# Grouped-query attention: a quarter of the score tiles get exp on VectorE, with the knot sum made by TensorE

## The chip, the cores and the metric

One core of a Trainium2 chip. The metric is the device time of one execution in microseconds; the number quoted for a kernel is the median of its runs. PE is TensorE, ACT is ScalarE, DVE is VectorE, POOL is GpSimd, SP is SyncE, whose queue issues DMAs. Differences between two changed kernels are of medians, and some of these come from different rounds; the kernel before ran in all of them, with medians from 545.3 to 547.2 us.

## The reference

```python
batch, n_q_heads, n_kv_heads, seq, head_dim = (8, 8, 2, 1024, 64)   # q, k, v: randn * 0.1, float32
for g in range(n_kv_heads):                       # 4 query heads share one k and v head
    scores = scale * q_group @ k_group.T          # scale = 1/8
    attn = exp(scores - scores.max(-1)); attn = attn / (attn.sum(-1) + 1e-08)
    output[:, q_start:q_end] = attn @ v_group
```

The inputs are small, so the scores are close to zero and the softmax is nearly uniform. A pass says little about how exact exp is.

## The kernel before

The work is cut into 64 units (batch, head pair, half of the queries) of 8 steps. A step is one chunk of 128 keys: PE makes its scores for two heads ("sides") in PSUM, ACT takes exp of three 512-column tiles at once, and ten steps later PE multiplies the result by V, with a column of ones appended that gives the softmax sum. V's matmuls use 64 key rows each, so that two of them (sides 0 and 1) run side by side in the array; half-way through a unit the sides swap, and a marker on SP's queue keeps the two row halves from touching one bank at once.

```python
    LAG = NKC + 2
    WIDTHS = (3, 3)                      # two score buffers of three banks
    def flush():
        pt = p_pool.tile([128, max(WIDTHS), QBS], BF16, name="pt")
        nc.scalar.activation(out=pt[...], in_=state["tile"][...], func=AF.Exp, scale=scale)
    def output_step(i):
        ...
        for c in (2 * part, 2 * part + 1):
            for qs in range(NQS):
                for rows in range(2):
                    side = rows ^ half
                    lo = rows * 64
                    mm = nc.tensor.matmul(ops[:, side, qs * (D + 1) : (qs + 1) * (D + 1)],
                        lhsT=pcell[(u * NKC + c, side)][lo : lo + 64, qs * 128 : (qs + 1) * 128],
                        rhs=vt[(b, side)][lo : lo + 64, c, :], ...)
        ...                              # end of a unit: reciprocal and multiply on DVE, from PSUM
        nc.vector.reciprocal(out=rec, in_=o[:, :, :, D])
        nc.vector.tensor_tensor(out=ost, in0=o[:, :, :, 0:D], in1=rec..., op=ALU.mult)
    # load_batch: GpSimd casts k and q to bf16 in DRAM, SP transposes them into SBUF by DMA (5 in a row)
```

The softmax here doesn't subtract the row's maximum and nothing guards it: scores larger than these inputs give would overflow.

## Time and profile before

| | before |
|---|---|
| median time | 546.68 us |
| ACT busy | 466.6 us (86%) |
| PE busy by the profile / at its real pace | 357.6 / about 240 us |
| DVE busy | 57.5 us |
| granted PE clock | 0.927 |

PE's list of waits (who waited, for whom: microseconds in all, how often, the longest):

```profile
PE sps L125 <- ACT pt L105: 99.8, 232, 1.1
PE ops L148 <- SPq L162: 36.1, 7, 10.4
PE ops L148 <- DVE ost L175: 22.8, 38, 1.0
```

PE mostly waits for ACT to free a score buffer. That is what a kernel bound by ACT looks like. The line of the normalisation (DVE ost) is small and its longest wait is 1.0 us: DVE has nothing else to do and serves at once.

### The profile page before, as it was taken

To read this page: it belongs to the slowest core of one execution; us is meant where nothing else is said; L and a number is where in the kernel's file an instruction comes from. 1 tells how busy PE (TensorE), PEld (TensorE's weight loads), DVE (VectorE), ACT (ScalarE), POOL (GpSimd) and SP (SyncE) were. 2 spreads that over 40 slices of the span, in tenths; PEclk is the share of its full clock that TensorE was granted. 3 is DMA by queue.
4 is the path that set the end of the run, shared out by engine and by line. 5 is a ranking of instruction groups with operands and counts; after the bars stand their busy time and mean duration, and the time that the engine had idled before them with its cause. 6 is when DMAs were issued, how large, how long until landed. Compare 5 with 4: busy or idle time off the path is not lost.

```text
span 545.4 us, 19767 instructions
## 1 busy us (share of the span) xinstructions
PE 357.6 (66%) x9216; PEld 228.7 (42%) x9216; DVE 57.5 (11%) x128; ACT 466.6 (86%) x343; POOL 98.2 (18%) x76
## 2 busy tenths in 40 slices
PE   0436766676748767587775767767674867767764
PEld 0024443444435444354443444444442544444443
DVE  0001011011101101011110110101110110111101
ACT  0547999699978999699996999959997899999994
POOL 8986100440007100080002600010000000000000
PEclk9988999699996999889996999869999699899999
DMA  9999923891159911698117921371114211111012
GB/s 75 156 149 157 157 45 69 114 132 40 32 111 97 97 41 43 117 115 83 40 33 127 132 47 41 68 109 41 41 37 99 45 39 41 41 42 40 22 41 61
DMA packets 209107, 41.13 MB, mean 75 GB/s; under 512 B 209024, under 2 KB 209024, under 8 KB 209024
## 3 DMA queue, kind: packets, MB, share of 16 engines
q0 software_dynamic: 99200, 12.59, 36.3%
q1 hardware_dynamic: 109824, 27.28, 26.0%
q8 instruction: 72, 1.18, 0.9%
q14 instruction: 11, 0.09, 0.1%
HBM read 25.17 MB, written 27.26 MB: 96 GB/s over the span
## 4 chain that ended last, share of the span: by engine, by line
ACT 45%; PE 21%; issue 13%; DVE 7%; SPq 7%; DMA 4%; POOL 3%; ACTq 0%; POOLq 0%
ACT pt L105 45%; PE ops L148 12%; PE sps L125 9%; SPq L81 6%; DVE ost L175 5%; DMA qscr<-in_q_dram 4%; POOL qscr L76 2%; DVE rec L173 2%; POOL kscr L67 1%; SPq L72 0%; POOL vs L86 0%; ACTq L105 0%; POOL vs L85 0%; SPq L162 0%; POOLq L215 0%
## 5 line engine op out<-in xcount | busy, mean ns | idle before, releaser
L105 ACT ACTIVATE pt<-sps 128x1536 bf16<-128x1536 f32 x342 | 465.3, 1472 | 70.8 <-PE sps L125 70.6
L125 PE MATMUL sps<-qT,kT 64*128 64x512 bf16 x1024 | 282.7, 410 | 121.4 <-ACT pt L105 99.8
L148 PEld LDWEIGHTS <-pt 64*128 64x128 bf16 x8192 | 217.0, 98 | 225.7 <-issue 83.8
L148 PE MATMUL ops<-vs,pt 64*128 64x65 bf16 x8192 | 260.0, 197 | 61.9 <-SPq L162 36.1
L125 PEld LDWEIGHTS <-kT 64*128 64x128 bf16 x1024 | 79.4, 99 | 86.4 <-issue 70.5
L76 POOL DMA_DIRECT2D qscr<-in_q_dram x32 | 72.0, 4055 | 3.8 <-DMA kscr<-in_k_dram 1.8
L173 DVE RECIPROCAL rec<-ops 128x8 f32<-128x8 f32 x64 | 13.3, 208 | 482.1 <-PE ops L148 482.1
L85 POOL MEMSET vs<- 128x8 bf16 x16 | 13.3, 833 | 251.3 <-PE ops L148 251.3
L175 DVE TENSOR_TENSOR ost<-ops,rec 128x512 f32<-128x512 f32 x64 | 44.2, 691 | 2.2
L67 POOL DMA_DIRECT2D kscr<-in_k_dram x8 | 16.5, 2058 | 0.9 <-POOLq L215 0.9
L86 POOL DMA_DIRECT2D vs<-in_v_dram x16 | 14.4, 897 | 9.6 <-POOL vs L85 5.9
L105 ACT ACT_TABLE_LOAD x1 | 1.3, 1283 | 0.7 <-PEq L215 0.7
L215 POOL MEMSET const-float32-0.0<- 128x1 f32 x1 | 0.1, 98 | 0.2 <-issue 0.2
L215 POOL MEMSET const-float32-1.0<- 128x1 f32 x1 | 0.1, 98 | 0.0
L215 POOL MEMSET const-bfloat16-1.0<- 128x1 bf16 x1 | 0.1, 98 | 0.0
L215 POOL MEMSET const-uint8-127<- 128x1 uint8 x1 | 0.1, 98 | 0.0
## 6 DMA issues: line engine op xcount, KB each, us to landing
out_dram<-ost SPq DMA_DIRECT2D x128, 128.0 KB, 2.2
qscr<-in_q_dram POOLq DMA_DIRECT2D x32, 256.0 KB, 12.6
kscr<-in_k_dram POOLq DMA_DIRECT2D x8, 256.0 KB, 6.2
vs<-in_v_dram POOLq DMA_DIRECT2D x16, 128.0 KB, 5.3
qT<-qscr SPq DMA_TRANSPOSE x32, 3.8
kT<-kscr SPq DMA_TRANSPOSE x8, 3.7
```

The source lines that it names most:

```text
L67: nc.gpsimd.dma_start(out=kscr.rearrange("s (g d) -> s g d", g=G), in_=k[b].rearrange("g s d -> s g d"),)
L76: nc.gpsimd.dma_start(out=qscr.rearrange("s (g d) -> s g d", g=G), in_=q[b, j::NPAIR].rearrange("g s d -> s g d"),)
L81: nc.sync.dma_start_transpose(out=qt, in_=qscr)
L85: nc.gpsimd.memset(vs[:, :, D], 1.0)
L86: nc.gpsimd.dma_start(out=vs[:, :, 0:D], in_=v[b, g].rearrange("(c p) d -> p c d", p=128),)
L105: nc.scalar.activation(out=pt[:, 0 : len(cells), :], in_=state["tile"][:, 0 : len(cells), :], func=AF.Exp, scale=scale,)
L125: nc.tensor.matmul(state["tile"][:, len(state["cells"]), :], lhsT=kT[b][side * D : (side + 1) * D, c * 128 : (c + 1) * 128], rhs=qT[(b, j) ...
L148: mm = nc.tensor.matmul(ops[:, side, qs * (D + 1) : (qs + 1) * (D + 1)], lhsT=pcell[(u * NKC + c, side)][lo : lo + 64, qs * 128 : (qs + 1) ...
L173: nc.vector.reciprocal(out=rec, in_=o[:, :, :, D])
L175: nc.vector.tensor_tensor(out=ost, in0=o[:, :, :, 0:D], in1=rec.unsqueeze(3).to_broadcast([128, G, NQS, D]), op=ALU.mult,)
L215: nc = _bacc.Bacc("TRN2", target_bir_lowering=False, num_devices=1)
```

## The change

The intent is to relieve ACT. On 4 of 15 steps DVE makes exp: one multiply-add turns the score into the bits of a bf16 number (so 2^x, linear between powers of two), written as uint16. Adding 32, 64 and 96 to those bits gives three more copies with shifted knots, and the weighted sum of the four is a much better exp. The sum costs no instruction of DVE: PE adds up four sets of output matmuls, each with its own weighted copy of V, which GpSimd prepares. Around this the change also makes the first transposes on PE, spreads the loads, uses score tiles of 1024 columns, and lets the output matmuls follow 15 steps behind, spread over 6.5 of 8 steps.

```diff
+KNOT_W = (1.0, 0.83984375, 0.70703125, 0.59375)
+KNOT_STEP = 32
-    LAG = NKC + 2
-    WIDTHS = (3, 3)
+    LAG = 15
+    GAP = 1.5
+    DVE_NUM, DVE_DEN = 4, 15
+    apool: 2 buffers of 2 banks (ACT);  dpool: 1 buffer of 2 banks (DVE);  ops: 2 banks      [summary]
+    def weigh_v(b, g):
+        for w in range(NK):
+            nc.gpsimd.tensor_scalar(out=vs[:, g, w, :, 0:D], in0=vf, scalar1=KNOT_W[w], ..., op0=ALU.mult)
+    def shift_knots():                   # for two DVE steps together
+        for w in range(1, NK):
+            nc.vector.tensor_scalar(out=pd[:, w, 0:n], in0=pd[:, 0, 0:n],
+                scalar1=float(w * KNOT_STEP), scalar2=None, op0=ALU.add)
     def score_step(i):
+        if not dve:
+            nc.scalar.activation(out=pt, in_=sps, func=AF.Exp, scale=scale)
+            pcell[i] = [pt]
+            return
+        nc.vector.tensor_scalar(out=pd[:, 0, n], in0=sps, scalar1=bits_scale, scalar2=bits_bias,
+            op0=ALU.mult, op1=ALU.add)
+        pcell[i] = [pd[:, w, n].bitcast(BF16) for w in range(NK)]
+        if n == 1:
+            shift_knots()
+    def output_items(u):
+        for half in range(2):
+            for c in range(NKC):
+                nk = NK if on_dve(u * NKC + c) else 1
+                items += [(half, c, w) for w in range(nk)]
+    # main loop: spread casts and transposes; score_step(i); then the output items due in step i;
+    # after the last item of a unit: reciprocal and multiply on DVE                           [summary]
```

## The prediction

> **What bounds the kernel now.** I read the page's totals first, then the groups, the waits of PE and ACT, the stretches by window, and the timeline of one good stretch, one batch change, and the end.
>
> ```profile
> PE 357.6 (66%) x9216; PEld 228.7 (42%) x9216; DVE 57.5 (11%) x128; ACT 466.6 (86%) x343; POOL 98.2 (18%) x76
> ...
> L105 ACT ACTIVATE pt<-sps 128x1536 bf16<-128x1536 f32 x342 | 465.3, 1472 | 70.8 <-PE sps L125 70.6
> ...
> L148 PE MATMUL ops<-vs,pt 64*128 64x65 bf16 x8192 | 260.0, 197 | 61.9 <-SPq L162 36.1
> L173 DVE RECIPROCAL rec<-ops 128x8 f32<-128x8 f32 x64 | 13.3, 208 | 482.1 <-PE ops L148 482.1
> L175 DVE TENSOR_TENSOR ost<-ops,rec 128x512 f32<-128x512 f32 x64 | 44.2, 691 | 2.2
> ```
>
> ACT does nothing but exp and is busy 466.6 of 545.4 us; it idles 70.8 us, all for scores from PE: 17.4 us of it before its first tile. DVE is busy for 11%. So exp on ACT bounds the steady stretch; some 53 us of stalls, about 19 us at the start and about 9 us at the end are added.
>
> ACT's pace, from its own timeline: seven tiles in one unbroken block.
>
> ```profile
> 19.41 9.51 ACT L105 ACTIVATE pt<-sps 128x1536 bf16<-128x1536 f32 x7 [17.39 <-PE sps L125]
> ```
>
> (9.51 - 1.47) / 6 = 1.34 us from start to start for 1536 columns: 0.833 ns a column and about 0.06 us fixed. The 1472 ns of the group is longer because neighbours overlap.
>
> PE's true pace also has to come from starts, since its ends are modelled. A good stretch (PE and its weight loads):
>
> ```profile
> 305.28 0.42 PE L148 MATMUL ops<-vs,pt 64*128 64x65 bf16 x16
> 305.50 0.10 PEld L125 LDWEIGHTS <-kT 64*128 64x128 bf16 x2
> 305.53 0.38 PE L125 MATMUL sps<-qT,kT 64*128 64x512 bf16 x2
> 305.53 0.50 PEld L148 LDWEIGHTS <-pt 64*128 64x128 bf16 x16
> 305.75 0.41 PE L148 MATMUL ops<-vs,pt 64*128 64x65 bf16 x16
> ```
>
> Sixteen output matmuls take 0.25 us (305.28 to 305.53), a pair of score matmuls 0.22 us (305.53 to 305.75). So PE's work is 512 steps x 0.47 = 240 us, far less than the 358 us "busy". A batch change shows what a PE stop costs:
>
> ```profile
> 292.49 0.62 PE L148 MATMUL ops<-vs,pt 64*128 64x65 bf16 x16 [3.76 <-SPq L162]
> 292.93 0.61 PE L125 MATMUL sps<-qT,kT 64*128 64x512 bf16 x2
> 293.33 0.65 PE L148 MATMUL ops<-vs,pt 64*128 64x65 bf16 x16
> ```
>
> After 3.76 us without work the same sixteen take 0.44 us and the pair 0.40; the stretches by window give a granted clock of 0.65, 0.50 and 0.83 from 290 to 305. The stop itself is the half-way marker of the output bank, which sits in SP's queue behind five DMA transposes of 1.25 us each.
>
> **What the Trainium skill says.** "TensorE: Matmul & The Clock Gate", HAM oscillation: an idle PE falls back to half clock; the trace agrees (0.50 above). "ScalarE: Activation LUTs", What ACT_TABLE_LOAD costs: 0.833 ns per element whatever the function; the trace agrees. "VectorE: DVE Perf Modes", The perf-mode tier table: a one-source 16-bit SBUF op of 2048 elements runs in the 4x mode in 693 ns, and a PSUM operand drops a tier; no run of before has such an op, so both figures for DVE are estimates. "SBUF — State Buffer", Who interferes with whom: a DVE op in a two-port mode and a GpSimd op lock each other out; before has no such DVE op.
>
> **The change, part by part.** 136 of 512 steps (a step is one key chunk of both heads, 128x1024 scores) go to DVE, 376 stay on ACT.
>
> *ACT.* One tile is now 1024 columns: 0.853 + 0.06 = 0.91 us. 376 x 0.91 = 343 us, from about 466: 120 us less.
>
> *DVE.* Conversion of 1024 columns from PSUM: the 128x512 multiply from PSUM takes 691 ns = 533 at one column a cycle + 158; for 1024, 1067 + 158 = 1.22 us. 136 x 1.22 = 166. Knot shifts: 68 groups x 3 x about 0.65 us (693 ns in isolation by the page, a little less back to back) = 133. Normalisation stays, 57.5. Sum about 357 us, from 57.5.
>
> *PE.* A DVE step needs four sets of output matmuls instead of one: 376 x 16 + 136 x 64 = 14720, from 8192. At the 64-in-1.04-us pace of the last unit's weight loads (16.2 ns each) that is 237 us, plus 512 x 0.22 = 113: 350 us at full clock, from 240.
>
> So the three engines stand at 343, 357 and 350 us. That is a balance on paper, but PE takes its instructions in order, ACT has two score buffers, DVE one, and there is one output bank pair; so what counts is what PE waits for.
>
> *The output turnover.* From the last output matmul of a unit to the first of the next: in the tail of before PE's last block ends at 537.41 (its last issue about 0.17 earlier), the reciprocal starts at 537.45, the multiply ends at 538.39, PE restarts at 538.44. That is 1.2 us of which two score pairs (0.44) of the new schedule fill a part, since the stream of output matmuls uses 6.5 of 8 steps. So 0.76 us of PE idle per unit, and per unit PE needs 14720/64 x 16.2 ns = 3.72 + 8 x 0.22 = 1.76: 5.48 + 0.76 = 6.24 us. ACT needs 5.36 us, DVE 5.6 us. PE's chain is the longest of the three.
>
> *The DVE queue in it.* DVE is in order too. If the second conversion of a pair has just been put in, the reciprocal waits behind a conversion and three shifts, 1.2 + 1.9 us. The pair's second step lies at steps 7 and 14 of 15, units end at step 6 of 8, so over 120 steps (15 units) every distance occurs twice: in the same step the reciprocal is about 2.6 us late, one step earlier 1.9, two 1.1, three 0.3, otherwise nothing. 2 x 5.9 / 15 = 0.8 us per unit on average if nothing absorbs it, and it comes in runs: about eight units with it, seven without.
>
> *Start.* K and the first Q come straight as fp32 and are transposed on PE in place of the cast to DRAM and the DMA transpose. 1 MB at the 157 GB/s seen in the first slices is 6.4 us, about 8.5 us with issue; then cast, 8 transposes, copy, about 3.5 us: first exp near 12.5 us instead of 19.4. The output stream starts 16.5 steps later, 11 us: about 24 us.
>
> *End.* Two units of output matmuls are left when scores are done: 2 x (3.7 + 1.2) = 10 us, and 3.6 us from the last multiply to the end as before.
>
> *Batch changes.* Transposes are spread four steps apart, so the marker no longer queues behind five of them; the 53 us of ACT stalls in the middle and the half clock after them go.
>
> *GpSimd.* 64 multiplies of 128x512 and the casts; busy for under a third of the span; can hold up a shift now and then, a few us.
>
> *Sum.* Without the DVE queue: 24 + 62 x 6.24 + 10 + 3.6 = 424 us. With all of it: 424 + 62 x 0.8 = 474 us. I take **445 us**, below the middle. The split at 4 of 15 and the stream's gap look chosen on a chip; if my queue were paid in full, fewer DVE steps would do better, so part of it is probably absorbed.
>
> **Rivals.**
> 1. *ACT or DVE stays the bound and the engines overlap nearly perfectly.* For: the sums of 343, 357 and 350 are so even, and the gap in the stream is about the turnover. 13 + 357 + 14 = 385 us. Against: PE in order, one output bank pair, one DVE score buffer; a step on DVE makes PE issue 0.22 + 0.52 us twice between two ACT tiles, 1.5 us, while ACT's two buffers allow little more than 1.1.
> 2. *PE's own clock.* Waits of 2.6 + 0.8 us come close to the 3.76 us that halved the clock in before. If each of some eight such places costs 5 us, and the mean clock stays near 0.93, PE's chain grows by 25 to 40 us: 485 to 500. For: the window table above. Against: two score pairs lie in the wait and PE is far denser elsewhere.
> 3. *The shifts don't run in the 4x mode* (uint16, with arithmetic), or GpSimd's lock holds them. At half rate a shift takes about 1.2 us, 204 of them 245 us, DVE 470 and with its waits about 510 us. Against: the skill's condition asks for 16-bit operands in SBUF with unit step, which these are.
> 4. *Nothing gained.* It would take rivals 2 and 3 together.
>
> **Range and chances.** The lower end, 408, is the sum without the queue and with part of the turnover hidden; the upper end, 490, is the full queue with some clock loss. Faster by over 2% means under 536 us: 94%. Within 2%: 4%. Slower: 2%; all of these belong to rivals 2 and 3 together.
>
> **What would show each step.**
> - ACT's tiles at a pace of 0.91 us and about 345 us busy; idle of 80 to 100 us, released by PE's scores.
> - DVE conversions near 1.2 us, shifts near 0.65 us; DVE busy about 355. A shift of 1.2 us would mean rival 3.
> - 14720 output matmuls, sixteen in about 0.26 us at full clock; PE's waits led by the multiply or reciprocal of the normalisation, some 45 to 100 us over 62 units, and not by SP's marker, which falls from 36 us (94 with the weight loads' waits) to little.
> - The waits at a unit's start in runs: about 60 steps with long ones, then about 60 with short ones. If they are even and short, the queue step is wrong.
> - Granted clock at or above 0.93; below that, rival 2.
> - First exp near 12 to 13 us; from last score to end about 14 us.
> - If PE's waits are mainly on ACT's score buffers, I have taken the wrong chain and rival 1 is the nearer one.

## The result, and the profile after

The change makes the kernel slower: 602.75 us against 546.68, ratio 1.101 (95% interval 1.097 to 1.106). The prediction said 445.

The page after, lines of totals, clock, the DMA queue that carries instructions, and groups (busy, mean ns of one, idle before):

```profile
PE 427.2 (71%) x15760; PEld 321.5 (53%) x15760; DVE 387.7 (64%) x471; ACT 368.8 (61%) x378; POOL 184.4 (31%) x120
...
PEclk9969799997878878999777897899978898999987
...
q8 instruction: 123, 2.02, 1.5%
...
L209 ACT ACTIVATE pa<-aps 128x1024 bf16<-128x1024 f32 x376 | 366.5, 1024 | 203.3 <-PE aps L200 201.5
...
L218 DVE TENSOR_SCALAR pd<-dps 128x1024 uint16<-128x1024 f32 x136 | 166.0, 1221 | 155.2 <-PE dps L200 154.9
...
L182 DVE TENSOR_SCALAR pd<-pd 128x2048 uint16<-128x2048 uint16 x204 | 169.2, 885 | 2.3
```

No engine is near its limit, ACT and DVE are idle for 203 and 155 us, and both idle for PE's scores. So PE is the one that stops. Its waits:

```profile
PE ops L249 <- DVE ost L267: 88.3, 58, 4.4
PE ops L249 <- issue: 49.9, 48, 2.5
PE aps L200 <- ACT pa L209: 8.9, 21, 0.9
...
PE ops L249 <- SPq L297: 4.8, 5, 2.6
PE dps L200 <- DVE pd L218: 4.1, 2, 2.6
```

Before, the first line was ACT's; now it is the normalisation, with a longest wait of 4.4 us in place of 1.0. And there is a new second line: 49.9 us of "issue", that is, no semaphore in the profile explains it. One place in the timeline shows both. PE:

```profile
296.87 1.12 PE L249 MATMUL ops<-vset,pd 64*128 64x65 bf16 x32
299.94 0.30 PE L249 MATMUL ops<-vset,pa 64*128 64x65 bf16 x8 [1.95 <-issue]
...
300.89 0.70 PE L200 MATMUL aps<-qT,kT 64*128 64x512 bf16 x4
304.55 0.68 PE L249 MATMUL ops<-vset,pa 64*128 64x65 bf16 x18 [2.96 <-DVE ost L267]
```

And DVE in the same window:

```profile
300.49 1.23 DVE L218 TENSOR_SCALAR pd<-dps 128x1024 uint16<-128x1024 f32 x1 [4.94 <-PE dps L200]
301.75 1.90 DVE L182 TENSOR_SCALAR pd<-pd 128x2048 uint16<-128x2048 uint16 x3
303.56 0.20 DVE L265 RECIPROCAL rec<-ops 128x8 f32<-128x8 f32 x1
303.80 0.69 DVE L267 TENSOR_TENSOR ost<-ops,rec 128x512 f32<-128x512 f32 x1
```

The unit's last output matmul is issued before 300.9. Its reciprocal could start at once, but conversion and three shifts stand in front of it on DVE until 303.56. PE comes back at 304.55, and the stretches by window give it a clock of 0.66 from 300 to 304 and 0.50 from 304 to 308.

To divide the span of 602 us I added up PE's matmuls from start to start. 398 us are dense work (350 at full clock by the prediction's durations), 98 us more are lost to the normalisation, 61 to issue, 16 to ACT's buffers, 7 to the half-way marker, 5 to DVE's score buffer; about 10 lie before the first and after the last matmul, and the remaining 6 belong to the first transposes. (These are a little above the profile's waits, because an idle PE's modelled end overlaps the next start.)

### The profile page after: what moved, and what is told of

Same layout as the page of the kernel before. It is cut to its first block, busy times and chain, and to the rows that moved or that the text cites. A ratio compares the mean times of both kernels' runs of the same rounds, so it can differ in the third digit from the quotient of the medians. Undisturbed runs are those within 1.5% of the kernel's fastest.

```text
span 601.9 us, 33347 instructions
## 1 busy us (share of the span) xinstructions
PE 427.2 (71%) x15760; PEld 321.5 (53%) x15760; DVE 387.7 (64%) x471; ACT 368.8 (61%) x378; POOL 184.4 (31%) x120
## 3 DMA queue, kind: packets, MB, share of 16 engines
q0 software_dynamic: 78432, 9.96, 27.4%
## 4 chain that ended last, share of the span: by engine, by line
PE 50%; DVE 27%; issue 12%; SPq 3%; DMA 3%; ACT 3%; POOL 2%; ACTq 0%
PE ops L249 36%; DVE pd L182 11%; PE aps L200 10%; DVE pd L218 7%; DVE ost L267 7%; PE dps L200 4%; ACT pa L209 3%; POOL vset L141 2%; DVE rec L265 2%; SPq L125 1%; DMA vstage<-in_v_dram 1%; DMA qscr<-in_q_dram 1%; SPq L132 1%; SPq L274 1%; DMA qT<-qscr 1%
## 5 line engine op out<-in xcount | busy, mean ns | idle before, releaser
L209 ACT ACTIVATE pa<-aps 128x1024 bf16<-128x1024 f32 x376 | 366.5, 1024 | 203.3 <-PE aps L200 201.5
L249 PE MATMUL ops<-vset,pd 64*128 64x65 bf16 x8704 | 237.5, 201 | 45.4 <-issue 29.8
L218 DVE TENSOR_SCALAR pd<-dps 128x1024 uint16<-128x1024 f32 x136 | 166.0, 1221 | 155.2 <-PE dps L200 154.9
L249 PE MATMUL ops<-vset,pa 64*128 64x65 bf16 x6016 | 179.4, 201 | 98.4 <-DVE ost L267 73.7
L249 PEld LDWEIGHTS <-pd 64*128 64x128 bf16 x8704 | 198.9, 101 | 86.7 <-issue 42.2
L249 PEld LDWEIGHTS <-pa 64*128 64x128 bf16 x6016 | 142.8, 101 | 143.2 <-DVE ost L267 81.3
L141 POOL TENSOR_SCALAR vset<-vstage 128x512 bf16<-128x512 f32 x64 | 105.9, 1655 | 317.4 <-DMA vstage<-in_v_dram 265.8
L182 DVE TENSOR_SCALAR pd<-pd 128x2048 uint16<-128x2048 uint16 x204 | 169.2, 885 | 2.3
L200 PE MATMUL aps<-qT,kT 64*128 64x512 bf16 x752 | 159.4, 419 | 13.0 <-ACT pa L209 8.9
L200 PE MATMUL dps<-qT,kT 64*128 64x512 bf16 x272 | 59.4, 420 | 4.4 <-DVE pd L218 4.1
```

Of the source, the lines that this page charges most:

```text
L141: nc.gpsimd.tensor_scalar(out=vs[:, g, w, :, 0:D], in0=vf, scalar1=KNOT_W[w], scalar2=None, op0=ALU.mult,)
L182: nc.vector.tensor_scalar(out=pd[:, w, 0:n], in0=pd[:, 0, 0:n], scalar1=float(w * KNOT_STEP), scalar2=None, op0=ALU.add,)
L200: nc.tensor.matmul(sps[:, side, :], lhsT=kT[b][side * D : (side + 1) * D, c * 128 : (c + 1) * 128], rhs=qT[(b, j)][side * D : (side + 1) * ...
L209: nc.scalar.activation(out=pt, in_=sps, func=AF.Exp, scale=scale)
L218: nc.vector.tensor_scalar(out=pd[:, 0, n], in0=sps, scalar1=bits_scale, scalar2=bits_bias, op0=ALU.mult, op1=ALU.add,)
L249: mm = nc.tensor.matmul(ops[:, side, qs * E1 : (qs + 1) * E1], lhsT=p[lo : lo + 64, side, qs * 128 : (qs + 1) * 128], rhs=vs[lo : lo + 64, ...
```

## The experiments

**Theories.** *Queue*: the normalisation stands behind conversion and shifts on DVE; PE, in order, stops for it, and its clock falls. *Load*: PE can't carry four sets of output matmuls. *Lock*: GpSimd stretches the shifts (885 ns on average where 693 is the median) and that is the harm. After the first four runs a fourth theory came in, *supply*: PE runs out of instructions.

| kernel | result | median, us | ratio to before | PE waits: normalisation / issue, us |
|---|---|---|---|---|
| before | right | 546.7 | 1 | 22.8 / 0.8 |
| the change | right | 602.8 | 1.101 | 88.3 / 49.9 |
| e1 shifts late | right | 560.0 | 1.025 | 29.1 / 61.2 |
| e2 no shifts | wrong | 557.5 | 1.022 | 36.8 / 78.9 |
| e3 one set | wrong | 523.8 | 0.961 | 95.9 / none |
| e4 none on DVE | right | 514.6 | 0.944 | 1.4 / none |
| e5 e1 + 128 rows | right | 510.9 | 0.934 | 27.4 / none |
| e6 e1, no loads after batch 0 | wrong | 483.1 | 0.883 | 27.8 / 32.0 |
| e7 e1, 2 of 15 | right | 497.0 | 0.908 | 14.9 / 19.0 |
| e9 e5, 2 of 15 | right | 467.1 | 0.855 | 15.6 / none |
| e10 e5, 1 of 10 | right | 480.8 | 0.880 | 11.2 / none |
| e11 e3 + shifts late | wrong | 471.5 | 0.864 | 28.0 / 1.0 |
| e12 e1, V not weighed | wrong | 544.9 | 0.997 | 30.3 / 68.0 |
| e13 128 rows, shifts early | right | 592.1 | 1.085 | 88.3 / none |
| e14 e5, 3 of 15 | right | 487.7 | 0.895 | 30.9 / none |
| e15 e1, no casts after batch 0 | passes, but uses batch 0's K and Q | 495.6 | 0.909 | 29.9 / 35.6 |

The issue column counts the lines of output matmuls; "none" means that the list of waits has no such line.

### e1: the shifts put in one by one

```diff
-        for w in range(1, NK):
-            nc.vector.tensor_scalar(...)          # three shifts at once, behind the conversion
+        shifts.extend((pd, n, w) for w in range(1, NK))
...
+            convert()                             # in a unit's last step: behind the normalisation
+            if i % NKC != 5:
+                one_shift()                       # one a step, none in the step before a unit's end
```

> Right result, same work: each of the three knot shifts is put in alone, one a step and none in the step before a unit ends, and a conversion in a unit's last step goes in behind the normalisation. Queue theory (PE stops because the normalisation stands behind conversion and shifts on DVE): PE's waits for the normalisation's multiply fall from 88 us to 40 to 55, the 3 to 5 us stops at unit starts go, the clock rises above 0.93, time 475 to 520 us. Load theory (PE cannot carry four sets of output matmuls and their instructions): the waits move elsewhere and the time stays above 575 us.

Measured: 559.97 us, 43 us less than the change, with the same instructions on every engine. PE's waits:

```profile
PE ops L263 <- issue: 61.2, 46, 4.2
PE ops L263 <- DVE ost L281: 29.1, 52, 1.0
PE dps L206 <- DVE pd L233: 16.6, 22, 2.5
```

The normalisation line fell from 88.3 to 29.1 us, even below what I expected, and its longest wait is back at the 1.0 us of before. The time from a unit's last output matmul to the next unit's first is 1.26 us on average instead of 2.20. So the queue was real. But the time missed my range by 40 us: issue grew to 61 us. A second cause was waiting behind the first.

### e2: no shifts at all

```diff
-        for w in range(1, NK):
-            nc.vector.tensor_scalar(...)
-        pcell[i] = [pd[:, w, n].bitcast(BF16) for w in range(NK)]
+        pcell[i] = [pd[:, 0, n].bitcast(BF16) for w in range(NK)]
```

> Wrong result on purpose: no knot shifts at all, the four output matmul sets read the same tile, so PE's work is unchanged and DVE loses 169 us. Queue theory: as with the shifts put late or a little better, 465 to 510 us, waits for the normalisation 40 to 55 us. Load theory: above 575 us. A GpSimd-lock theory (shifts stretched from 0.69 to 0.89 us by GpSimd are the harm) expects this one to be fast and the late shifts to stay slow.

Measured: 557.53 us, the same as with the shifts late, although DVE is now busy for 221.9 us instead of 382.3.

```profile
PE ops L241 <- issue: 78.9, 62, 6.1
PE ops L241 <- DVE ost L259: 36.8, 54, 1.3
```

So taking the shifts away brings nothing beyond putting them elsewhere. The lock theory expected this kernel to be much faster than e1, and falls in that form. But supply hides something here: from start to start, the waits for DVE's score buffer, 21 us in e1, are gone in e2, and issue takes 21 us more. What long shifts cost in a kernel that supply does not hold was not tested; in e11 below PE's longest line is for DVE's score buffer (45.2 us). My range (465 to 510) was missed for the same reason as in e1.

### e3: one set of output matmuls

```diff
-                nk = NK if on_dve(u * NKC + c) else 1
+                nk = 1
```

> Wrong result on purpose: one output matmul set for a DVE step instead of four, 8192 matmuls as before the change; DVE's work unchanged. Queue theory: PE still waits 60 to 90 us for the normalisation, time 460 to 510 us, since DVE's queue is as long. Load theory: the waits shrink to under 40 us and the time falls to 400 to 440 us, near DVE's and ACT's sums.

Measured: 523.82 us.

```profile
PE ops L249 <- DVE ost L267: 95.9, 58, 5.5
PE aps L200 <- ACT pa L209: 31.2, 82, 0.7
PE dps L200 <- DVE pd L218: 22.3, 17, 5.3
```

The normalisation waits stay (95.9 us) with the matmuls of before, as the queue theory said. And the issue line is gone altogether, with 72 packets on the instruction queue instead of 123. The time came 14 us over my range, the waits 6 us.

### e4: nothing on DVE

```diff
-    DVE_NUM, DVE_DEN = 4, 15
+    DVE_NUM, DVE_DEN = 0, 15
```

> Right result: all score tiles on ACT, the rest of the change kept (start through PE transposes, spread loads, 1024-column tiles, output stream). Both theories: ACT-bound, 512 x 0.91 = 467 us busy with start and tail about 495 us (485 to 515), so the rest of the change alone is a gain and the DVE share is what costs over 90 us.

Measured: 514.59 us, as expected: the rest of the change is worth 6% against before. PE waits for ACT again, as it should in a kernel bound by ACT:

```profile
PE aps L200 <- ACT pa L209: 128.9, 408, 0.7
PE ops L249 <- SPq L297: 20.0, 11, 3.9
```

So the DVE share of 4 of 15, meant as the gain, costs 88 us.

### What "issue" is: reading the trace again

In the change's trace 44 issue gaps of PE are longer than 0.4 us. Counted in matmuls, the first come at numbers 991, 1247, 1631, 1887, 2015: a multiple of 128 apart, and over the whole run the place in the 128 drifts by only seven. A matmul and its weight load are two instructions, so that is every 256 instructions. The instruction queue of the DMA page moved 123 packets of 16384 bytes. The Trainium skill, Perfetto Trace Analysis, The 4-stage abstract model, gives 64 bytes for an instruction, and 256 x 64 is 16384. Each of the 44 gaps ends 1.2 to 1.7 us after such a packet has landed. In both traces, before and after, two packets never start closer together than 3.38 us. PE needs 2 us for 128 output matmuls at full clock.

That gives the supply theory: PE's instructions come in pieces of 256, one every 3.35 us or so at best (the least in any run is 3.24), and dense stretches of small matmuls run dry.

### e8: PE alone

```diff
+        for n in range(1024): rows64(n == 0)        # 8 output matmuls of 64 rows each time
+        for n in range(1024): rows128(n == 0)       # 8 of 128 rows
+        for n in range(256): scores(); rows64(False); rows64(...)
+        for n in range(256): scores(); rows128(...)
```

> Wrong result on purpose, PE alone on constant data, no waits: 8192 output matmuls of 64 rows, then 8192 of 128 rows, then 256 times a score pair with sixteen 64-row ones, then 256 times a score pair with eight 128-row ones. Supply theory: the first part takes 64 pieces x 3.4 = 215 us (26 ns each) with a gap at every piece, although sixteen take 0.25 us inside a piece; array-load theory: 8192 x 16.2 ns = 133 us without gaps. The 128-row part is expected at 27 to 30 ns each; the difference of the last two parts tells what changing the row mode costs.

The timeline of its first part (no other engine runs, no DMA but instructions):

```profile
11.01 2.14 PE L60 MATMUL ops<-vs,p 64*128 64x65 bf16 x128 [0.72 <-issue]
14.46 2.14 PE L60 MATMUL ops<-vs,p 64*128 64x65 bf16 x128 [1.31 <-issue]
17.91 2.15 PE L60 MATMUL ops<-vs,p 64*128 64x65 bf16 x128 [1.31 <-issue]
```

Exactly 128 matmuls, 1.31 us of nothing, 128 matmuls, 3.46 us from one to the next. 8192 matmuls take 226.5 us, 27.6 ns each, though each takes 15.7 ns inside a piece. (I had expected 215 us, and 133 without the limit.) So the supply limit is shown, by itself, without the loads or the other engines. The 128-row matmuls take 31.1 ns each, a little over my 27 to 30, without a gap: at that pace 128 of them outlast a piece. They do twice the work of one 64-row matmul, so the array works as fast and needs half the instructions. The last two parts give what changing the row mode costs: a score pair with sixteen 64-row matmuls 0.50 us, with eight 128-row ones 0.677 us, of which 0.22 + 8 x 0.031 = 0.47 is work: 0.21 us for going and coming back. The skill, TensorEngine Tiling (Array Packing), Key Properties, says that changing the mode drains TensorE; 0.21 us is what two changes cost here.

### e5: 128-row output matmuls

```diff
-            for rows in range(2):
-                side = rows ^ half
-                lo = rows * 64
+            for side in range(2):
-                    lhsT=p[lo : lo + 64, side, qs * 128 : (qs + 1) * 128],
-                    rhs=vs[lo : lo + 64, side, w, c, :],
+                    lhsT=p[:, side, qs * 128 : (qs + 1) * 128],
+                    rhs=vs[:, side, w, c, :],
```

> Right result; on top of the late shifts the output matmuls take all 128 key rows at once, so 7360 of them instead of 14720 pairs of half the rows, at the same array time (65 columns against two halves side by side), and no half-way marker. Supply theory (PE's instructions arrive in pieces of 256, one every 3.35 us at best; 123 pieces need 412 us): 66 pieces, PE's waits put down to issue fall from 67 us to under 15, time 470 to 520 us if changing between 64-row and 128-row matmuls costs under 0.1 us each way; if changing is dear (0.2 us each way, 512 times) the issue waits still go but the time stays near 560 us. Array-load theory: issue waits stay, time within 2% of 560 us.

Measured: 510.86 us, 49 us less than e1 and inside my range, although PE now changes its row mode 435 times each way (counted in the trace; some score pairs follow each other, so it is not the 512 of the expectation). At e8's price that is an estimated 91 us of extra time.

```profile
PE ops L260 <- DVE ost L275: 27.4, 50, 1.5
PE dps L206 <- DVE pd L233: 15.3, 19, 2.1
```

No issue line is left, and the instruction queue moved 65 packets. PE's dense work is 430 us from start to start, about the sum of 113 for scores, 7360 x 31.1 ns = 229 and these 91. The array-load theory is out.

### e6, e12, e15: what makes pieces late

On top of the 3.35 us some pieces are late: e1's longest issue gap is 4.2 us. Three kernels take away parts of what runs on GpSimd and the DMA queues.

```diff
 e6:  batches 1 to 7 use batch 0's K, Q and V: no casts, transposes, loads or weighing
 e12: -                if at in (28, 32):
      -                    weigh_v(b + 1, (at - 28) // 4)      (all batches use batch 0's weighed V)
 e15: V loaded and weighed; K and Q of batches 1 to 7 neither cast nor transposed
```

> Wrong result on purpose: the late shifts, and batches 1 to 7 reuse batch 0's K, Q and V, so that GpSimd and the load DMAs are quiet after the first 40 us. Supply theory: the pieces still come no closer than 3.35 us, but none is late behind loads, so issue waits of over 2 us go and those of about 1 us stay: 15 to 40 us in all, time 510 to 540 us. GpSimd-lock theory: shifts all at 0.69 us and the time falls below 500 us because of it. Array-load theory: no change, 550 to 560 us.

> Wrong result on purpose: late shifts, casts and transposes of all batches kept, but V is not weighed on GpSimd after batch 0. If the loads' DMA traffic makes instruction pieces late, issue waits stay above 50 us and the time at 530 to 560 us. If GpSimd's multiplies were what the quiet run lost, shifts fall to near 0.72 us and the time to 483 to 510 us.

> Wrong result on purpose: late shifts, V loaded and weighed for all batches, but K and Q of batches 1 to 7 neither cast nor transposed. If casts and transposes make the pieces late: issue waits 25 to 40 us, none over 2 us, time 485 to 510 us, shifts at 0.75 to 0.8 us. If GpSimd's weighing was the harm of the two: above 530 us.

e6: 483.1 us, 77 us less than e1 and 27 us better than my range; in time alone it is what the GpSimd-lock theory expected.

```profile
PE ops L263 <- issue: 32.0, 46, 1.5
PE ops L263 <- DVE ost L281: 27.8, 49, 1.0
```

The pieces come no closer (3.31 us at least, 3.62 in the median), but the longest gap is 1.5 us. The clock is 0.992 instead of 0.934, and PE's dense work fell from 382 to 357 us with it. The shifts are at 705 ns, as the lock theory said too, but PE's waits for DVE's score buffer, where long shifts would show, fell only from 16.6 to 9.3 us.

e12 was not the clean test I wanted: without the weighing GpSimd ran ahead and put all casts into the first 120 us. (Its time, 544.9 us, and its issue waits, 68.0 us, are what I had given for late pieces through DMA traffic.) The run does concentrate the effect, though. Its DMA view from 44 to 124 us:

```profile
DMA  9999999999999999999999999999999999999992
...
q8 instruction: 12, 0.20, 0.9%
```

With the DMA engines full of casts, pieces start 7.0 us apart on average; from 130 us on, 3.85. There are 12 issue gaps in it, one for each piece, of 0.5 to 4.5 us and 2.5 us on average. No weighing runs in that stretch.

e15: 495.6 us, with all weighing kept.

```profile
PE ops L263 <- issue: 35.6, 49, 1.8
```

So it is the casts and transposes: taking them away gives 64 of the 77 us that e6 gave. About 29 of the 64 are shorter issue waits in all PE's lines, and 27 are dense work at the higher clock (0.992); waits for DVE's score buffer fell by 4. The time and the shifts (761 ns) are in my range; one issue gap, in front of a score matmul, is 2.1 us, just over my limit. Which of the two makes the pieces late I haven't separated, but in e12's stretch the casts' queue alone fills the engines (its packets overlap to 164% of them, the other queue's to 36%).

### e11 and e13: the two causes apart

```diff
 e11: e3's one set, with e1's late shifts
 e13: e5's 128 rows, with the shifts early as in the change
```

> Wrong result on purpose: late shifts and one output matmul set for a DVE step, the missing corner of a square with the change (603 us), the late shifts (560) and one set alone (524). Queue theory: normalisation waits fall from 96 to under 40 us and the time to 435 to 475 us, so that the queue is worth more where supply does not bind. If the two effects simply add, 481 us. If PE's load alone mattered, it stays at 515 us or more.

> Right result: the change as it is, shifts early, but output matmuls of 128 rows, so half the instructions. If queue and supply are two separate causes: issue waits go, normalisation waits stay at 80 us or more, time 545 to 585 us, 35 to 70 us above the same with late shifts (511). If supply alone explained the loss, about 511 us.

| | shifts early | shifts late | queue costs |
|---|---|---|---|
| four sets, 64 rows (supply binds) | 602.8 | 560.0 | 43 |
| four sets, 128 rows | 592.1 | 510.9 | 81 |
| one set, 64 rows | 523.8 | 471.5 | 52 |

e13 keeps the whole normalisation wait, with no issue line beside it:

```profile
PE ops L246 <- DVE ost L261: 88.3, 59, 4.9
```

Both causes act by themselves, and they overlap: with the shifts early, halving the instructions brings only 11 us (592.1 against 602.8), with the shifts late 49. These are net figures. From start to start the issue waits that go are 62 us with the shifts early and 79 with them late, while PE's dense work, with the row mode changing, rises by 61 and 50 us; the clock is lower with the shifts early (0.919 in e13, 0.986 in e5), which makes dense work longer. For the smaller issue wait with shifts early, a natural reading is that while PE stands at the normalisation its next pieces arrive; I have not tested that. The queue's 81 us in the second row are 64 us of waits at the normalisation and 28 of dense work, less 12 of waits for DVE's score buffer. e13 landed 7 us over my range, e11 inside it.

### e7, e14, e9, e10: the share

```diff
-    DVE_NUM, DVE_DEN = 4, 15
+    DVE_NUM, DVE_DEN = 2, 15        # e7 on e1; e9 on e5; e14: 3, 15 and e10: 1, 10, both on e5
```

> Right result: the late shifts with 2 of 15 steps on DVE. 98 pieces x 3.4 = 333 us, ACT 444 x 0.91 = 404 us, DVE about 208 us: ACT becomes the bound again with waits; both theories expect a time below 4 of 15 and below none, 455 to 500 us.

> Right result: late shifts, 128-row matmuls, 3 of 15 on DVE. PE 113 + 107 + 6544 x 31 ns = 423 us is the bound: 480 to 495 us, between 2 of 15 (467) and 4 of 15 (511).

> Right result: late shifts, 128-row output matmuls, 2 of 15 steps on DVE. PE: 512 x 0.22 scores + 512 x 0.21 changes of row mode + 5728 x 31 ns = 398 us; ACT 444 x 0.91 = 404 us; supply no longer binds. Supply and queue theories: 450 to 480 us, under the 497 us of the 64-row form. If supply was not what held the 64-row form, no better than 497 us.

> Right result: the same with 1 of 10 steps on DVE: ACT 461 x 0.91 = 420 us becomes the clear bound, PE 385 us: 455 to 485 us, within 2% of 2 of 15; if it is the faster one, ACT's tolerance for a late score tile, and not its sum, sets the best share.

All four came inside their ranges of time; e10 is 2.9% above e9, where I expected them within 2%. With 128 rows and late shifts: 510.9 at 4 of 15, 487.7 at 3, 467.1 at 2, 480.8 at 1 of 10 (e10's PE and DVE work is less than e9's, yet it is slower; ACT has more, 431 against 417 us, and PE waits 47 us for its buffers against 33, so ACT is the likely reason). The best kernel is e9, correct, 14.5% faster than before (ratio 0.855, 0.852 to 0.857) and 22% below the change's time. Its totals and first waits:

```profile
PE 402.5 (87%) x6768; PEld 256.7 (55%) x6768; DVE 221.1 (48%) x301; ACT 416.7 (90%) x446; POOL 180.7 (39%) x120
```

```profile
PE aps L206 <- ACT pa L215: 32.6, 107, 0.8
PE ops L260 <- DVE ost L275: 15.6, 29, 1.4
```

ACT is at 90%, and PE's first wait is for ACT's buffers, as in the kernel before, but 80 us sooner.

## Why the prediction was wrong

*What held.* The durations: conversions 1221 ns (predicted 1220; with 691 ns for 512 columns that is 1.04 ns a column), shifts 693 ns in the median, which is the figure of the skill's page that the prediction names, and three in 1.90 us, 14720 output matmuls, ACT's tiles from start to start 0.91 us, first exp at 13.3 us (12.5). The balance of sums: ACT 367 (343), DVE 388 (357), and PE 355 to 357 of dense work in the runs with a clock of 0.992 (350). The chain was the right one too: PE's waits are led by the normalisation.

*The queue step held in size.* Predicted per unit: 1.2 us turnover and 0.8 us of queue, 2.0 together. Measured: 2.20 us on average over 63 units, and in runs: units 14 to 19 and 29 to 35 wait 2.6 to 5.2 us, units 23 to 28 and 38 to 43 mostly 1.22. PE lost 98 us to it; the undiscounted prediction had 62 x (0.76 + 0.8) = 97.

*The step that failed first* is the last of the sum: "I take 445 us, below the middle. [...] part of it is probably absorbed." The reason given was that the split of 4 of 15 looked chosen on a chip. Nothing in the profile said so, and it was wrong twice: nothing was absorbed, and 4 of 15 is not the best share: e4, with none on DVE, is 88 us faster than the change, and e7, with 2 of 15, 63 us faster than e1. The full sum stood there, 474. But this step is worth only 29 us; the full sum was itself 128 us short.

*The step that failed most* is PE's term, "14720 [...] at the 64-in-1.04-us pace [...]: 350 us at full clock", taken as a pace that PE keeps. It measured 398 us of dense work and 61 of issue, 459 in all. From 474 to the span of 602 us 128 are missing, and these two parts are 109 of them. PE's dense work is 398 us, not 350: 48 us for the half clock, which was my rival 2, given as 25 to 40 us and then left out of the sum. Quiet runs (e6, e15) at a clock of 0.992 have 355 to 357 us of dense work, so the term is the clock's. The change's own trace agrees: where the granted clock is 0.5 its 2929 matmuls without a wait take 36.5 ns each from start to start, where it is 1.0 they take 21.3, and the difference makes an estimated 45 us. 61 us are the instruction supply, which no step and no rival named. It was there to be seen in principle: the page of before lists 72 instruction packets for 9216 matmuls, and the change adds 6528 matmuls; but before's own pace is a packet every 6.6 us in the median, and only its last two come as close as 3.40 us, so no wait showed the limit. The remaining 19 us or so are small waits (ACT's buffers 16, the marker 7, DVE's score buffer 5) less what the 24 us of the start already held.

*The pace was read from too short a stretch.* "Sixteen in 0.25 us" is right for sixteen, and right for the 64 of the tail that I used. It does not hold for a longer stream: e8's first part runs dry after every 128.

Two small slips in its sums change nothing: 13 + 357 + 14 is 384, and the 1.05 MB of the first K and Q take 6.7 us at 157 GB/s.

*Rivals.* Rival 1, near-perfect overlap, was far off. Rival 3 in its first form, no 4x mode, didn't happen; in its second, GpSimd holding the shifts, it did (0.885 us on average, 1.8 when a cast was being issued, about 40 us of DVE's time in all where the prediction had "a few us"). In e2 taking the shifts away brought nothing over e1, but supply held both. Rival 2 came, at 48 us. Rival 4, nothing gained, is what happened, though "rivals 2 and 3 together" would not have been enough: the instruction supply is in neither.

*Chances.* 94% for a gain, and 2% for the loss that came, rested on sums that left slack for one of these terms but not for three together.

## What to carry to other kernels

When work moves to an engine that also does a small job on another engine's critical turn, look at the order in its queue, not at its total: a conversion and three shifts in front of a 0.9 us normalisation cost 43 to 81 us here, and with the shifts put in one at a time PE's waits for it were back at 27 to 29 us in the correct kernels with 4 of 15 steps on DVE, against 23 before the change. Count the instructions as well as the array time of PE; a stream of small matmuls can run out of instructions, and the same work with twice the rows needs half of them.

## What the Trainium skill lacked or had wrong

- No page gives a rate at which an engine's instructions are supplied. Runtime: NRT & Kernel Launch, Instruction fetch mechanics, describes the blocks of 256 instructions and calls the cost of going from one to the next mostly hidden. Here it was not: PE gets 256 instructions (one packet of 16384 bytes) every 3.3 to 3.5 us when it runs dry, so that load and 64-row matmul pairs of 65 columns sustain 27.6 ns instead of 15.7 (e8). With the DMA engines full of casts the pieces came 7.0 us apart (e12).
- TensorE: Matmul & The Clock Gate, Back-to-back issue gap, gives about 81 ns per matmul as the sustained rate of load and matmul pairs at 128 columns. No run here has a stream of that shape, but at 65 columns e8 sustained 27.6 ns (64 rows) and 31.1 ns (128 rows), so that figure can't be taken over for narrower pairs.
- TensorEngine Tiling (Array Packing), Key Properties, names the drain at a change of tiling mode but no price: 0.21 us for going to 128 rows and back (e8).
- SBUF — State Buffer, Who interferes with whom, tells that a DVE op in a two-port mode and a GpSimd op lock each other out, whoever issues second waiting; for the writing of DMA descriptors it names only GpSimd as the side that starves. Here the DVE side paid: shifts of 0.69 us took 1.8 us on average while GpSimd was issuing a cast, and 0.98 us beside its weighing. The issue of a Q cast took 3.61 us on average, and 3.63 in e2, where no shifts run.
